# Spreading a row of reciprocal roots over the partitions: through DRAM instead of through TensorE

## The chip, the cores and the metric

The kernel runs on one core of one Trainium2 chip, as one launch. The metric is the device time of that core in microseconds, the median of several executions. One further execution is taken with the hardware profiler; its rows are what is read here. PE is TensorE (PEld its weight loads), DVE is VectorE, ACT is ScalarE, POOL is GpSimd, and SPq is the queue on which SyncE issues transfers.

## The reference, cut to what matters

Two layers of a transformer trunk, with 1024 tokens and a width of 1024, in float32. In each layer three groups of heads attend in their own ways, and each group's output is normalised by itself before the output projection:

```python
for l in range(DEPTH):
    h = rms_norm(x, g_attn[l]) * (1 + sc_a) + sh_a
    qa, ka, va, qb, kb, vb, qc, kc, vc = split_cols(h @ w_in[l], IN_SPLITS)
    ya = neighborhood_attention(...)       # 4 heads, two-dimensional window
    yb = sliding_window_attention(...)     # 6 heads, a band of 128 either way
    yc = axial_attention(...)              # 6 heads, dense
    ga, gb, gc = split_cols(g_group[l], GROUP_WIDTHS)      # widths 256, 384, 384
    y = jnp.concatenate([rms_norm(ya, ga), rms_norm(yb, gb), rms_norm(yc, gc)], axis=-1)
    x = x + gt_a * (y @ w_o[l])
    ...                                    # SwiGLU part, then the next layer

def rms_norm(x, g):
    y = x * lax.rsqrt(jnp.mean(x * x, axis=-1, keepdims=True) + EPS)
    return y * g
```

## The kernel before, in words

Features lie on the 128 partitions and tokens along the free dimension. The attention output is the tile `y`, eight chunks of 128 features by 1024 tokens: chunks 0 and 1 are the two-dimensional group, 2 to 4 the band group, 5 to 7 the dense group. A group's norm needs one factor per token, the same on all partitions.

The attention part is a list of 64 pairs (a head and two blocks of 128 queries): 24 dense ones, 16 of the two-dimensional group, 24 of the band group. A loop over the step `n` works on several pairs at once. For the last 40 pairs, which this text calls the attention band, step `n` computes the scores of pair `n`+4 (PE into `sA` or `sB`; DVE adds the bias from `zA` or `bz` and takes the extreme into `rs`), the exponentials of the pair scored a step earlier (ACT), the division of the one before that (`scale_rows` on `pr`, POOL), turns pair `n` by PE transposes into `T` (copied out as `pt` and `edge`), and multiplies pair `n`-2 with the values into `pv`. Two pairs share one `pv`; ACT copies half of it to `cmb` and DVE adds both into `y`, so DVE writes `y` once per two pairs.

A norm goes along beside that. As heads end, POOL squares and sums (`norm_sum`: `gsq` into `gss`). A list `later` holds callables by step. When a group's last head is done, at step `n` (24 for the dense group, 42 for the two-dimensional one), `stats` is put at `n`+5: PE sums `gss` over the partitions into `ps_st`, and DVE takes the reciprocal root by Newton steps (`isq`), which leaves `rstd`, 128 x 8: token 128j + p in column j of partition p. At `n`+8 `scale` calls `norm_scale`: for each half of 512 tokens `spread` transposes four columns of `rstd`, broadcast to 128 x 128, into one PSUM bank (`ps_r`), and ACT copies it to `rb`, 128 x 512, with the same row on each partition. The multiplies of `y` by `rb`, one per chunk and half, are put one per step from `n`+9, on POOL: six for the dense group, four for the two-dimensional one. The band group's norm comes after the loop and goes through the same `norm_scale`.

What orders the work: on PE, ACT and DVE the loop's own instructions are pinned, which means that they are held in written order; POOL is pinned throughout the loop; what `later` issues on PE, ACT and DVE is not pinned, and from step 6 SP isn't either. What is not pinned is placed by the framework's planner, which takes it up when it expects it to be ready. Each queue then executes in the order that was planned.

The transfers on SP in the band: the heads' `q` and `k` from `qkd` into `qk` tiles (two buffers). Group 0 of the band group is made in step 32 and group 1 in step 36, with five transfers of 512 KB each, when the `qk` tile of a head of the two-dimensional group comes free. The bias tiles `bz` come one per head, and the rows of `w_o` for the projection that follows (`wst`). Near the end of the band, `y_split` (ACT and DVE, into `yq`, a `qk` tile) makes two-part copies of scaled chunks, and parts of the projection (`ps_o`) are mixed in.

All instructions of the trace carry line 49, that of the helper that records them, so they are told apart by their tiles.

Of the kernel before, what the change touches and what calls it, by code (L numbers as in the profile page):

```python
# [10 lines left out]
F32 = mybir.dt.float32  # L11
# [3 lines left out]
ALU = mybir.AluOpType  # L15
# [4 lines left out]
P = 128  # L20
D = 1024
S = 1024
KC = D // P
H = 512
# [56 lines left out]
def bc(ap, shape):  # L81
    return ap.to_broadcast(shape)
# [3 lines left out]
def trunk(ctx: ExitStack, tc, A, C, out):  # L86
    nc = tc.nc
    pe, act, dve, pool, sp = (
        Engine(tc, e) for e in (nc.tensor, nc.scalar, nc.vector, nc.gpsimd, nc.sync)
    )  # L90
# [5 lines left out]
    def open_pool(name, bufs=1, side="left", space=None):  # L96
        kw = dict(name=name, bufs=bufs, side=side, reuse_waits="tile")
        if space is not None:
            kw["space"] = space
            if space == PSUM:  # L100
                kw.pop("side")
        cm = tc.tile_pool(**kw)
        p = cm.__enter__()
        return cm, p
# [10 lines left out]
    dp = ctx.enter_context(tc.tile_pool(name="dram", bufs=1, space=DRAM))  # L115
# [23 lines left out]
    skA = [dp.tile([4, P, 512], F32, name=f"skA{l}") for l in range(2)]  # L139
    vAd = dp.tile([S, 4 * P], F32, name="vAd")  # L140
    rowB = dp.tile([6, 512], F32, name="rowB")
    skB = dp.tile([6, P, 512], F32, name="skB")

    gpd = dp.tile([P, 7 * NB, H], F32, name="gpd")
# [177 lines left out]
    todo = [(0, g) for g in (2, 3, 4, 5)] + [(1, g) for g in range(6)]  # L322
# [114 lines left out]
    def spread(r, j0, psp, tag="mm"):  # L437

        ps = psp.tile([P, 512], F32, name="ps_r", tag=tag)
        for j in range(4):  # L440
            pe.transpose(
                ps[:, j * P : (j + 1) * P], bc(r[:, j0 + j : j0 + j + 1], [P, P]), ident
            )
        return ps
# [406 lines left out]
    rb = stp2.tile([P, H], F32, name="rb", tag="rb", bufs=2)  # L851
# [116 lines left out]
    rb = stp2.tile([P, H], F32, name="rb", tag="rb", bufs=2)  # L968
# [37 lines left out]
    for l in range(2):  # L1006
# [403 lines left out]
        for oc in range(NE, 8):  # L1410
            w = wab
            for half in range(2):
# [16 lines left out]
                i = 2 * (oc - NE) + half  # L1429
# [17 lines left out]
        y = yp.tile([P, 8, S], F32, name="y")  # L1447
        ap_cm, app = open_pool("apad", side="right")
        pad(app, 32)
        at_cm, atp = open_pool("att", side="right")  # L1450
        psT_cm, psT = open_pool("psT", bufs=PS_T, space=PSUM)
# [276 lines left out]
        class PairA(Band):  # L1728


            name, by_columns = "sA", True
# [11 lines left out]
        class PairB(Band):  # L1743
            name = "sB"
# [12 lines left out]
        def norm_sum(chunks, ss, last, half, late):  # L1757
# [14 lines left out]
            square(sq)  # L1772
            pool.tensor_tensor(out=ss[:, c], in0=ss[:, c], in1=sq, op=ALU.add)

        def norm_scale(chunks, r, psp, tag, engines):

            todo = []
            for half, eng in enumerate(engines):
                c = slice(half * H, (half + 1) * H)
                ps = spread(r, 4 * half, psp, tag=tag)  # L1780
                rb = atp.tile([P, H], F32, name="rb", tag="rb", bufs=2)
                act.copy(rb, ps)
                for n in chunks:
                    todo.append(
                        lambda eng=eng, n=n, c=c, rb=rb: eng.tensor_tensor(
                            out=y[:, n, c], in0=y[:, n, c], in1=rb, op=ALU.mult
                        )
                    )
            return todo

        korder = (5, 6, 7, 0, 1, 2, 3, 4)
# [59 lines left out]
        later = {}  # L1851
# [6 lines left out]
        for n in range(-AHEAD - 1, N + 3):  # L1858
# [84 lines left out]
            for end, (chunks, width) in norms.items():  # L1943
                if begins[end] <= m <= end and (m - begins[end]) % 8 == 7 and (n <= NC or m >= NC):
                    i = (m - begins[end]) // 8
                    if end not in gss:
                        gss[end] = gss_tile()
                    for half in range(2):
                        what = lambda a=(chunks, gss[end], i, half, m == N - 1): norm_sum(*a)
                        if m == N - 1:  # L1950
                            what()
                        else:
                            later.setdefault(n + 1 + half, []).append(what)
                    if m == end and end < N - 1:

                        def stats(end=end, width=width, n=n, chunks=chunks):
                            r = rstd_cols(
                                gss[end], width, 8, atp, psT, tag="T", newton=True, turned=False
                            )

                            def scale():
                                todo = norm_scale(chunks, r, psT, "T", (pool, pool))
                                for i, what in enumerate(todo):
                                    later.setdefault(n + 9 + i, []).append(what)

                            later.setdefault(n + 8, []).append(scale)

                        later.setdefault(n + 5, []).append(stats)
            pin((pe, act, dve), n < 0 or n >= NC - 1)
# [33 lines left out]
        for ki in range(5):  # L2003
# [8 lines left out]
            if ki == 2:  # L2012
                r = rstd_cols(gss[N - 1], norms[N - 1][1], 8, atp, psl, newton=True, turned=False)
# [316 lines left out]
        for q in range(NF):  # L2330
# [4 lines left out]
            if q < EARLY:  # L2335
                up = q % 2
                e = sg[q // 2][0][:, 0:H]
                if up:
                    (pool if q > 1 else dve).tensor_tensor(
                        out=e, in0=e, in1=quads[q]["11"], op=ALU.mult  # L2340
# [196 lines left out]
        for u in range(NU):  # L2537
            i, t = divmod(u, NB)
# [34 lines left out]
            if t < NB - 1:  # L2573
                continue
            m, half = {
                1: (0, 0), 2: (0, 0), 6: (0, 1), 7: (1, 1), 4: (1, 0), 5: (1, 1), 3: (0, 1),
            }[num]
# [29 lines left out]
        if last_layer:  # L2607
# [5 lines left out]
            r = ntp.tile([P, 8], F32, name="rstd", tag="rstd", bufs=2)  # L2613
# [122 lines left out]
```

## Time and profile before

| | us |
|---|---|
| median of 3 runs | 2355.33 (2355.26 to 2355.58) |
| profiled execution, time | 2355.82 |
| its span, first to last instruction | 2354.0 |
| granted TensorE clock, mean | 0.999 |
| `ps_r` transposes, `rstd` and identity, x72 | 0.273 each |
| copies `rb` from `ps_r` on ACT, x14 | 0.587 each |
| multiplies of `y` by `rb` on POOL, x26 | 1.290 each |

The span is what the rows add up to; the profiled execution took 1.8 us more than its span. Of the 72 transposes, 48 belong to the three group norms of two layers (eight each). A timeline row gives the start, the duration, the engine, the operation, the written and read tiles, the shapes and, in brackets, the idle time before it and what ended that. A row of a stretch gives the length, the busy time of PE, PEld, DVE, ACT and POOL with the number of instructions, the granted clock, the mean busy share of the 16 DMA engines, and the GB/s. A row of a transfer's tile view gives the minimum, median and maximum duration of its issue in ns, and the line under it the time from issue to landing. Layer 0's attention band lies at about 357 to 465 us of the span, layer 1's at about 1508 to 1616.

### The profile page before, as it was taken

To read this page: it belongs to the slowest core of one execution; us is meant where nothing else is said; L and a number is where in the kernel's file an instruction comes from. 1 tells how busy PE (TensorE), PEld (TensorE's weight loads), DVE (VectorE), ACT (ScalarE), POOL (GpSimd) and SP (SyncE) were. 2 spreads that over 40 slices of the span, in tenths; PEclk is the share of its full clock that TensorE was granted. 3 is DMA by queue.
4 is the path that set the end of the run, shared out by engine and by line. 5 is a ranking of instruction groups with operands and counts; after the bars stand their busy time and mean duration, and the time that the engine had idled before them with its cause. 6 is when DMAs were issued, how large, how long until landed. Compare 5 with 4: busy or idle time off the path is not lost. (4 is left out here: it accounts for less than half of the span.)

```text
span 2354.0 us, 33488 instructions
## 1 busy us (share of the span) xinstructions
PE 2320.3 (99%) x11825; PEld 1956.5 (83%) x11825; DVE 1737.0 (74%) x2720; ACT 1185.5 (50%) x2264; POOL 792.0 (34%) x758
## 2 busy tenths in 40 slices
PE   9999999999999999999999999999999999999998
PEld 7888898888788888888888889988878888888887
DVE  7866998869867777495777579897796664537865
ACT  5423888845543333344633168896454333334444
POOL 1530447610344444100145124574005443430021
PEclk9999999999999999999999999999999999999999
DMA  8676316163435444785434851332633443339633
GB/s 282 182 224 220 120 30 190 44 219 94 137 131 166 157 139 152 216 249 181 152 102 140 252 175 28 93 104 94 216 103 128 150 156 103 103 99 295 215 112 121
DMA packets 306168, 357.49 MB, mean 152 GB/s; under 512 B 51892, under 2 KB 223772, under 8 KB 306000
## 3 DMA queue, kind: packets, MB, share of 16 engines
q1 hardware_dynamic: 289504, 345.74, 46.5%
q10 hardware_dynamic: 16128, 9.44, 1.5%
q8 instruction: 93, 1.52, 0.3%
q14 instruction: 75, 0.61, 0.1%
q0 software_dynamic: 368, 0.17, 0.0%
HBM read 270.32 MB, written 88.63 MB: 152 GB/s over the span
## 5 line engine op out<-in xcount | busy, mean ns | idle before, releaser
L49 PE MATMUL ps_d<-wpt 128*128 128x512 f32 x1848 | 425.2, 390 | 0.8 <-ACT hh L49 0.2
L49 PEld LDWEIGHTS ps_d<-wpt 128*128 128x128 f32 x1848 | 345.4, 188 | 75.4 <-issue 1.9
L49 POOL TENSOR_SCALAR pr<-pr,rs 128x1024 f32<-128x1024 f32 (+2 forms) x248 | 190.8, 784 | 189.4 <-DVE rs L49 172.2
L49 POOL TENSOR_TENSOR sg<-sg,u 128x512 f32<-128x512 f32 x82 | 118.7, 1447 | 344.1 <-ACT sg L49 219.8
L49 PE MATMUL pv<-pt,vs 128*128 128x256 f32 x1088 | 174.0, 296 | 14.4 <-DVE y L49 13.1
L49 ACT COPY u<-ps_w 128x512 f32<-128x512 f32 x128 | 75.1, 587 | 213.5 <-PE ps_w L49 213.5
L49 DVE TENSOR_TENSOR pt<-T,pt 128x512 fp32r<-128x512 f32 x272 | 177.3, 679 | 7.0 <-ACT pt L49 5.8
L49 POOL TENSOR_TENSOR wpt<-ws,wpt 128x512 fp32r<-128x512 f32 x80 | 110.8, 1386 | 205.2 <-ACT wpt L49 152.0
L49 ACT CAST pt<-T 128x512 fp32r<-128x512 f32 x272 | 151.6, 586 | 42.3 <-PE T L49 40.9
L49 DVE TENSOR_TENSOR wpt<-w,wpt 128x512 fp32r<-128x512 f32 x154 | 110.3, 717 | 79.8 <-ACT wpt L49 79.6
L49 PEld LDWEIGHTS pv<-pt,vs 128*128 128x128 f32 x1088 | 141.0, 189 | 27.2 <-DVE y L49 25.2
L49 ACT CAST wpt<-w 128x512 fp32r<-128x512 f32 x154 | 95.6, 620 | 132.2 <-PE ps_d L49 124.7
L49 PE MATMUL T<-identr,pr 128*128 128x128 f32 x1176 | 159.9, 273 | 1.0 <-DVE pt L49 0.6
L49 PEld LDWEIGHTS T<-identr,pr 128*128 128x128 f32 x1176 | 137.8, 140 | 15.7 <-ACT edge L49 1.0
L49 DVE SCALAR_TENSOR_TENSOR acc<-wmt,condT,acc 128x512 f32<-128x512 f32 (+1 forms) x92 | 104.8, 1149 | 62.0 <-DMA wmt<-in_w_mod_dram 61.6
L49 ACT CAST wpt<-ws 128x512 fp32r<-128x512 f32 x176 | 107.2, 619 | 56.5 <-PE ps_w L49 26.7
L49 ACT CAST wpt<-graw 128x512 fp32r<-128x512 f32 x154 | 95.0, 617 | 72.5 <-DMA graw<-gpd 68.4
L49 DVE TENSOR_TENSOR wpt<-ws,wpt 128x512 fp32r<-128x512 f32 x96 | 83.1, 873 | 53.1 <-ACT wpt L49 52.8
L49 DVE TENSOR_TENSOR wpt<-graw,wpt 128x512 fp32r<-128x512 f32 x154 | 112.0, 727 | 11.7 <-ACT wpt L49 11.7
L49 DVE TENSOR_REDUCE rs<-sC 128x1 f32<-128x1024 f32 x88 | 107.4, 1220 | 12.7 <-PE sC L49 11.5
L49 DVE TENSOR_TENSOR ws<-wr 128x512 f32<-128x512 f32 x88 | 81.8, 930 | 41.3 <-POOL wpt L49 38.0
L49 DVE TENSOR_TENSOR wlo<-wst,whi 128x1024 fp32r<-128x1024 f32 (+1 forms) x71 | 92.6, 1308 | 25.1 <-ACT whi L49 21.7
(314 smaller groups left out, 5943.1 us busy)
## 6 DMA issues: line engine op xcount, KB each, us to landing
wr<-in_w_gu_dram SPq DMA_DIRECT2D x92, 512.0 KB, 4.1
gpd<-sg SPq DMA_DIRECT2D x154, 256.0 KB, 4.4
graw<-gpd SPq DMA_DIRECT2D x76, 512.0 KB, 3.5
w<-in_w_down_dram SPq DMA_DIRECT2D x110, 256.0 KB, 4.7
wmt<-in_w_mod_dram SPq DMA_DIRECT2D x48, 512.0 KB, 5.2
qk<-qkd SPq DMA_DIRECT2D x44, 512.0 KB, 7.2
wst<-in_w_o_dram SPq DMA_DIRECT2D x32, 512.0 KB, 4.2
wmt<-in_w_mod_dram SPq DMA_DIRECT2D x64, 256.0 KB, 3.9
```

What stands on the lines that cost most here:

```text
L49: ins = op(*args, **kwargs)
```

## The change

For the dense and the two-dimensional group, `rstd` no longer goes through PE, PSUM and ACT. At `n`+8 SP stores it to a DRAM row of 1024 elements (`rowN`), at `n`+9 SP loads each half of that row to all 128 partitions of an `rb` tile, and the multiplies, still on POOL, are put from `n`+12. The band group's norm keeps `norm_scale`.

```diff
     rowB = dp.tile([6, 512], F32, name="rowB")
+    rowN = dp.tile([S], F32, name="rowN")
...
+        def scaled(chunks, half, rb, eng):
+
+            c = slice(half * H, (half + 1) * H)
+            return [
+                lambda n=n: eng.tensor_tensor(
+                    out=y[:, n, c], in0=y[:, n, c], in1=rb, op=ALU.mult
+                )
+                for n in chunks
+            ]
+
+        def rb_tile():
+            return atp.tile([P, H], F32, name="rb", tag="rb", bufs=2)
+
         def norm_scale(chunks, r, psp, tag, engines):
 
             todo = []
             for half, eng in enumerate(engines):
-                c = slice(half * H, (half + 1) * H)
                 ps = spread(r, 4 * half, psp, tag=tag)
-                rb = atp.tile([P, H], F32, name="rb", tag="rb", bufs=2)
+                rb = rb_tile()
                 act.copy(rb, ps)
...
+                todo += scaled(chunks, half, rb, eng)
+            return todo
+
+        def rows_store(r):
+            sp.dma_start(rowN.rearrange("(j p) -> p j", p=P), r)
+
+        def rows_load(chunks):
+            todo = []
+            for half in range(2):
+                rb = rb_tile()
+                row = rowN[half * H : (half + 1) * H]
+                sp.dma_start(rb, bc(row[None, :], [P, H]))
+                todo += scaled(chunks, half, rb, pool)
             return todo
...
                             def scale():
-                                todo = norm_scale(chunks, r, psT, "T", (pool, pool))
-                                for i, what in enumerate(todo):
-                                    later.setdefault(n + 9 + i, []).append(what)
-
-                            later.setdefault(n + 8, []).append(scale)
+                                for i, what in enumerate(rows_load(chunks)):
+                                    later.setdefault(n + 12 + i, []).append(what)
+
+                            later.setdefault(n + 8, []).append(lambda: rows_store(r))
+                            later.setdefault(n + 9, []).append(scale)
```

More of the change, by code (lines that the diff above doesn't have):

```diff
@@ L1778, in norm_scale @@
             for half, eng in enumerate(engines):
-                c = slice(half * H, (half + 1) * H)
                 ps = spread(r, 4 * half, psp, tag=tag)
-                rb = atp.tile([P, H], F32, name="rb", tag="rb", bufs=2)
+                rb = rb_tile()
                 act.copy(rb, ps)
[L1783 to L1788, printed above, removed]
+                todo += scaled(chunks, half, rb, eng)
[9 more added lines that the diff above has]
+                todo += scaled(chunks, half, rb, pool)
             return todo
```

## The prediction

> **What bounds the kernel now.** I read the page first (engines, chain, DMA queues), then the busy time by stretch around the places that change, then the order of events there.
>
> ```profile
> span 2354.0 us, 33488 instructions
> ...
> PE 2320.3 (99%) x11825; PEld 1956.5 (83%) x11825; DVE 1737.0 (74%) x2720; ACT 1185.5 (50%) x2264; POOL 792.0 (34%) x758
> ...
> q1 hardware_dynamic: 289504, 345.74, 46.5%
> q10 hardware_dynamic: 16128, 9.44, 1.5%
> ```
>
> TensorE is busy for 99% of the span, so over the whole program it is the bound, and any TensorE work that goes away can shorten it. The span average hides the attention band, though, where the edit lies:
>
> ```profile
> core 0: us, PE busy (x) PEld busy (x) DVE busy (x) ACT busy (x) POOL busy (x), PEclk, DMA share, GB/s
> 381.00:390.50 9.50, 9.11 (x72) 8.44 (x71) 8.11 (x29) 8.95 (x25) 6.82 (x10) 1.00 0.94 275
> 391.50:400.60 9.10, 8.64 (x67) 8.05 (x66) 8.15 (x26) 8.77 (x26) 9.10 (x15) 1.00 0.97 283
> 425.00:437.00 12.00, 9.34 (x75) 8.70 (x73) 11.76 (x32) 11.77 (x32) 9.55 (x13) 1.00 0.07 19
> ```
>
> At the first norm (chunks 5 to 7) PE and ACT are nearly full, and ten microseconds later POOL is full without a gap. The DMA engines are also full through both stretches. At the second norm (chunks 0 and 1) DVE and ACT are full, PE isn't, and DMA is idle. So the four places (two norms in two layers) have two different prices.
>
> **What is removed.** Per changed norm, two halves of four transposes and one copy:
>
> ```profile
> L49 PE MATMUL ps_r<-identr,rstd x8: 271/273/273, 384.0 to 384.8; 128*128 128x128 f32 x8
> L49 ACT COPY rb<-ps_r x2: 575/584/592, 384.7 to 385.2; 128x512 f32<-128x512 f32 x2
> ...
> 384.02 1.04 PE L49 MATMUL ps_r<-identr,rstd 128*128 128x128 f32 x8
> 428.57 1.04 PE L49 MATMUL ps_r<-identr,rstd 128*128 128x128 f32 x8
> 1535.54 1.04 PE L49 MATMUL ps_r<-identr,rstd 128*128 128x128 f32 x8
> ```
>
> That is 1.04 us of PE for eight pipelined transposes (with their eight weight loads beneath) and about 1.06 us of ACT, four times in all. What a place is worth can be read from the beat of the loop. DVE writes one `y` per two pairs:
>
> ```profile
> 381.89 0.69 DVE L49 TENSOR_TENSOR y<-pv,cmb 64x512 f32<-64x512 f32 x1
> 387.46 0.69 DVE L49 TENSOR_TENSOR y<-pv,cmb 64x512 f32<-64x512 f32 x1 [0.20 <-ACT cmb L49]
> 391.99 0.68 DVE L49 TENSOR_TENSOR y<-pv,cmb 64x512 f32<-64x512 f32 x1
> 396.68 0.68 DVE L49 TENSOR_TENSOR y<-pv,cmb 64x512 f32<-64x512 f32 x1 [0.19 <-ACT cmb L49]
> ```
>
> The beats are 5.57, 4.53 and 4.69 us; the first contains the transposes. Against the mean of the other two (4.61) it is 0.96 us long, so nearly all of the 1.04 us is on the path: gain 0.95 at the first norm. One pair (one step `n`) is thus 2.3 us. At the second norm DVE is busy 11.76 of 12.00 us, so taking work from PE and ACT can give no more than DVE's free 0.24 us as long as DVE's own work stays; the other end would be the full 1.04. I take 0.2, since DVE is the nearer limit. Over two layers: 2 x 0.95 + 2 x 0.2 = 2.3 us gained if nothing new is waited for.
>
> **What is added.** Four stores (1024 elements of 4 bytes each, strided) and eight loads (128 partitions x 2 KB, all from one row) on SP, 12 issues. A store waits for `rstd`; both loads wait for the store to land, and whatever SP holds behind them waits too. The multiplies by `rb` stay on POOL, same count and size, but three steps later (`n`+12 for `n`+9). POOL's order is fixed, so a late `rb` also holds the divisions of `pr` that stand behind it, and PE's transposes of `pr` wait for those. What is just then on the DMA queue is the heart of it:
>
> ```profile
> 383.73 0.16 DVE L49 SCALAR_TENSOR_TENSOR rstd<-isq,rstd 128x8 f32<-128x8 f32 x1
> ...
> L49 SPq DMA_DIRECT2D qk<-qkd x5: 430/580/598, 379.8 to 382.1; - x5
> DMA to landing us min/median/max: 4.8/9.1/9.8
> ...
> L49 SPq DMA_DIRECT2D qk<-qkd x5: 430/580/607, 389.8 to 392.2; - x5
> DMA to landing us min/median/max: 5.1/7.4/8.1
> ...
> L49 SPq DMA_DIRECT2D qk<-qkd x5: 430/580/609, 1531.3 to 1533.7; - x5
> DMA to landing us min/median/max: 5.0/7.0/8.6
> ...
> L49 SPq DMA_DIRECT2D qk<-qkd x5: 430/579/614, 1541.3 to 1543.7; - x5
> DMA to landing us min/median/max: 6.2/8.8/9.6
> ...
> bz<-skB SPq DMA_DIRECT2D x12, 192.0 KB, 2.3
> skB<-rowB SPq DMA_DIRECT2D x6, 256.0 KB, 10.3
> ```
>
> `rstd` is ready at 383.9. The five 512 KB loads of group 0 were issued from 379.8 to 382.1 and land one after another, the last 9.8 us after 382.1, at 391.9: the later the issue, the longer the landing, which is a queue served in order. I take it that the store, issued at 384 on the same queue, lands behind them. Its own transfer isn't in the trace. Queue q1's packets took 46.5% of 16 x 2354 us for 289504, or 60.5 ns each (mean 1.2 KB), q10's 1.5%, or 35 ns each (585 B). With 1024 packets over 16 engines that is 64 x 60.5 = 3.9 us at the upper end and next to nothing at the lower; nearest are q10's small packets, 2.2 us, and since 4 B is far less than 585 B I take half, 1.1. So the store lands at 393.0. Then a load: the quiet 192 KB `bz` took 2.3 us, and 256 KB at that rate of growth some 2.6 (upper end: the broadcast `skB` loads, six in a row, 10.3). So `rb` is there at L = 395.6.
>
> The Trainium skill (DMA: Bandwidth & Descriptors, Rules for kernel authors) says that a strided last dimension becomes one descriptor per element, and its Measured table gives about 10.5 ns a packet: 64 x 10.5 = 0.67 us, an estimate, which would put the sum below 0.4 us lower in each layer. No run here shows such a store.
>
> **When POOL needs it.**
>
> ```profile
> 385.38 1.29 POOL L49 TENSOR_TENSOR y<-y,rb 128x512 f32<-128x512 f32 x1 [0.20 <-ACT rb L49]
> 390.58 0.18 POOL L49 COPY pr<-sinkc 128x2 f32<-128x2 f32 x1
> 391.98 1.03 POOL L49 TENSOR_TENSOR gss<-y 128x512 f32<-128x512 f32 x1
> 400.05 1.28 POOL L49 TENSOR_TENSOR y<-y,rb 128x512 f32<-128x512 f32 x1
> 401.32 1.15 POOL L49 TENSOR_SCALAR pr<-pr,rs 128x384 f32<-128x384 f32 x2
> ...
> 390.97 0.83 PE L49 MATMUL sB<-qk 128*128 128x256 f32 x4
> 403.79 0.81 PE L49 MATMUL T<-identr,pr 128*128 128x128 f32 x6
> 410.20 0.71 PE L49 MATMUL T<-identr,pr 128*128 128x128 f32 x5
> ```
>
> A step costs POOL 1.1 (division) + 0.18 (sink) + 1.29 (multiply) = 2.6 us against a beat of 2.3, so POOL falls behind while the multiplies last; a division is used two steps later. Now the sixth multiply's next division ends at 401.32 + 1.15 = 402.5 for a transpose of pair 41 at 403.79: 1.3 us to spare, no more. After the change the train of six multiplies starts three steps later. From its first start at L, POOL does 6 multiplies, one `gss` and 6 divisions with 5 sinks before the last division it delays: 7.7 + 1.0 + 6.6 + 0.9 = 16.2 us. That one belongs to pair 44, transposed at 410.20, or 409.2 with 0.95 taken off. So L may be 393.0. (The first sB at 390.97 is pair 40, scored at step 36; counting on gives the pairs.) At 395.6 PE stalls 2.6 us. In layer 1 everything stands 1151.5 later (1535.54 against 384.02), but group 0's last load lands at 1533.7 + 8.6 = 1542.3 instead of 1543.4, 1.1 earlier: stall 1.5.
>
> At the second norm DMA is at a share of 0.07: store from 428.6, 2.6 + 2.6 us plus issues, `rb` near 435. Its multiplies start at step 54, four steps after the store's step, some 9 us: hidden. The `bz` load queued beside it has ten steps before its own use. Group 1's loads behind the first norm's wait are used from step 48, and are late without harm. Were these covers gone, it would cost the same microsecond for microsecond.
>
> **Sum.** -2.3 + 2.6 + 1.5 = +1.8 us. The profiled execution took 2355.82 around a span of 2354.0, 0.5 above the median of 2355.33 (2355.26 to 2355.58); on the median it gives 2357.1. About 0.2% (4.7 us) is what a measurement here can tell from no change, so this is no change.
>
> **Rivals.**
>
> *The loads stand behind group 1 on SP (slower).* SP's order is set ahead by a planner. Group 1 is free to go at 389.8, before the store has landed (393.0); if the planner sees that, its five loads go first. For it: ready first. Against it: the `rb` loads come three steps earlier in the program. Then L is group 1's last landing, 392.2 + 8.1 = 400.3, less 0.95, plus about 1 for the load itself: 400.4, a stall of 7.4; in layer 1, 1553.3 + 0.05 against 1544.5: 8.9. Sum 16.3 - 2.3 = +14.0, 2369.3. It decides from the point where group 1's first issue precedes the `rb` loads.
>
> *The small writes are slow (slower).* At 60.5 ns a packet the store takes 3.9 instead of 1.1, L grows by 2.8 in both layers, +1.8 + 5.6 = +7.4: 2362.7. For it: nothing in this trace writes 4-byte pieces. Against it: smaller packets are cheaper in the two queue rows. The Trainium skill (DMA: Bandwidth & Descriptors, Specifications) speaks for this one: below 512 B it says the engine reads, modifies and writes. No run here shows it.
>
> *The transfers are hidden (no change).* If the store is not held by group 0, it lands about 387 and `rb` about 390, before 393.0: -2.3, 2353.0; with the whole 1.04 at the second norms too, -4.0, 2351.3. Against it: the rising landing times.
>
> *More than the removed work comes back (faster).* If both the PE and the ACT microsecond lie on the path at all four places, because the planner lays out the unpinned splits around 425 anew, 4 x 2.1 = 8.4: 2346.9. Against it: DVE at 11.76 of 12.00.
>
> **How the numbers follow.** My forecast 0.32, hidden 0.20, behind group 1 0.24, slow writes 0.12, more comes back 0.12. The likeliest gives 2357.1, its own range 2354 to 2360. Faster by over 0.2% is only the last: 0.12. Slower is the two slow ones plus a little of my own range's upper part: 0.38. The rest, 0.50, is within. The range for 8 in 10 leaves out the faster case and the far end of the slow one: 2350.5 to 2371.
>
> **What would show it.** Right: the transposes and copies of `rstd` are gone at four places of six; the beat at 381.9 falls to 4.6; the store lands 8 to 9 us after its issue in the first norms and 2 to 4 in the second; POOL waits for DMA `rb` about 4 us once per layer, and PE's T waits for POOL `pr`, 2.6 and 1.5 us. Wrong: no wait of POOL for `rb` (hidden), one of some 9 us with group 1 issued ahead (behind group 1), or a store that lands long after group 0 (slow writes). Gains elsewhere would mean a new layout by the planner, which I can't read from this trace.

## The result, and the profile after

The changed kernel takes 2390.72 us, the median of 4 runs (2386.55 to 2393.56), where the kernel before, timed beside it on the same chip, takes 2355.30 (2355.07 to 2355.58). The ratio is 1.0147, with a 95% interval of 1.0135 to 1.0158: 35 us slower. I had forecast 2357.1, no change, in a range that ended at 2371.0. The profiled execution took 2388.63 around a span of 2386.4, 32.4 more than the span before; the accounts below are made on the spans.

The page after, its span and its engines:

```profile
span 2386.4 us, 33424 instructions
...
PE 2326.6 (97%) x11793; PEld 1962.3 (82%) x11793; DVE 1734.2 (73%) x2720; ACT 1182.6 (50%) x2256; POOL 793.0 (33%) x758
```

PE has 32 instructions fewer and is busy a little longer (2326.6 us, 2320.3 before); it stands idle for 60 us of the span instead of 34. So 26 of the 32.4 us are waiting. What SyncE's queue issued in layer 0, around the two changed norms (start, duration, queue):

```profile
384.29 0.37 SPq L49 DMA_DIRECT2D rowN<-rstd  x1
389.30 0.58 SPq L49 DMA_DIRECT2D qk<-qkd  x1
398.56 2.45 SPq L49 DMA_DIRECT2D rb<-rowN  x2
...
438.00 0.37 SPq L49 DMA_DIRECT2D rowN<-rstd  x1
447.08 0.32 SPq L49 DMA_DIRECT2D rb<-rowN  x1
```

The store of the dense norm's factors was issued at 384.29, where I had put it. The two loads of `rb` could only be issued once it had landed, and that was at 398.56, not at 393.0. One of group 1's `qk` loads went between; the other four went behind. At the second norm the same store takes from 438.00 to 447.08, 9.1 us, for 4 KB (in layer 1 from 1605.99 to 1616.63, 10.6 us). Busy time by stretch after (columns as in the prediction):

```profile
402.00:406.00 4.00, 0.24 (x1) 0.24 (x2) 0.00 (x0) 0.00 (x0) 3.12 (x4) 0.50 0.94 185
438.00:440.00 2.00, 2.00 (x19) 2.00 (x18) 2.00 (x7) 2.00 (x6) 1.31 (x4) 1.00 0.23 2
440.00:441.00 1.00, 1.00 (x11) 0.97 (x9) 0.91 (x5) 0.97 (x4) 1.00 (x2) 1.00 0.00 0
...
452.00:456.00 4.00, 0.33 (x1) 0.18 (x1) 0.98 (x3) 2.91 (x8) 4.00 (x6) 0.92 0.04 14
```

The second row is the second store at work: 0.23 of 2 us on 16 engines is 1024 packets of 4 bytes at 7 ns each, and the trace has all of them between 438.91 and 439.59. From 440 to 441 the DMA share is 0.00, and yet the store lands only at 447.0. So its packets take 0.7 us, and the 7.4 us behind the last of them, which show as no DMA work, are what the loads wait for. Other transfers are slow beside it: two packets of 8 KB on another queue that start in that time (441.4 and 442.5) take 3.06 us each, where two such packets took 0.31 and 0.49 us in the kernel before (433.1 and 433.8). The first and the last row show what the late stores cost: from 402 to 406 and from 452 to 456, PE did 0.24 and 0.33 us of work in 4 us. The order of events there, at the first norm:

```profile
402.88 1.26 POOL L49 TENSOR_TENSOR y<-y,rb 128x512 f32<-128x512 f32 x1 [10.37 <-DMA rb<-rowN]
...
405.76 1.36 PE L49 MATMUL T<-identr,pr 128*128 128x128 f32 x5 [7.29 <-POOL pr L49]
...
418.58 0.84 PE L49 MATMUL sB<-qk 128*128 128x256 f32 x4
```

POOL waited 10.37 us for `rb`, and PE behind it 7.29 us for the division `pr` that stands behind the multiply in POOL's order. The row `sB` at 418.58 is pair 48. Before, the same pair, pair 52 and the first product of the output projection that reads `y` stood here:

```profile
409.53 0.83 PE L49 MATMUL sB<-qk 128*128 128x256 f32 x4
...
420.53 0.84 PE L49 MATMUL sB<-qk 128*128 128x256 f32 x4
...
507.19 0.39 PE L49 MATMUL ps_o<-y,whi 128*128 128x512 f32 x1
```

So layer 0's first norm costs 418.58 - 409.53 = 9.05 us. And the second norm after, with the same product:

```profile
451.77 1.26 POOL L49 TENSOR_TENSOR y<-y,rb 128x512 f32<-128x512 f32 x1 [5.04 <-DMA rb<-rowN]
...
453.07 0.72 ACT L49 ACTIVATE qk<-y,vecs 128x512 fp32r<-128x512 f32 x1 [5.34 <-POOL y L49]
...
455.67 0.47 PE L49 MATMUL T<-identr,pr 128*128 128x128 f32 x1 [4.92 <-ACT edge L49]
...
522.56 0.39 PE L49 MATMUL ps_o<-y,whi 128*128 128x512 f32 x1
```

POOL waits 5.04 us for `rb`; ACT waits 5.34 us for POOL's product `y`, because the split of that chunk (`qk<-y,vecs`) stands in ACT's order ahead of work that the loop needs; PE waits 4.92 us for ACT's `edge`. By that product layer 0 has lost 522.56 - 507.19 = 15.37 us, so the second norm's share is 6.3. Layer 1 repeats it, first before, then after:

```profile
1561.04 0.84 PE L49 MATMUL sB<-qk 128*128 128x256 f32 x4
```

```profile
1570.85 1.26 POOL L49 TENSOR_TENSOR y<-y,rb 128x512 f32<-128x512 f32 x1 [11.01 <-DMA rb<-rowN]
...
1573.72 1.36 PE L49 MATMUL T<-identr,pr 128*128 128x128 f32 x5 [7.93 <-POOL pr L49]
...
1586.52 0.83 PE L49 MATMUL sB<-qk 128*128 128x256 f32 x4
```

Pair 48 of layer 1 is 25.48 us late, 10.1 more than layer 0 had lost; the last product of the projection that reads `y` in layer 1 is 31.4 late (1703.17 before, 1734.57 after). That accounts for 9.05 + 6.3 + 10.1 + 5.9 = 31.4 of the 32.4 us.

### The profile page after: what moved, and what is told of

The parts are those of the page before. It is cut to its first block, busy times and chain, and to the rows that moved or that the text cites. A ratio compares the mean times of both kernels' runs of the same rounds, so it can differ in the third digit from the quotient of the medians.

```text
span 2386.4 us, 33424 instructions
## 1 busy us (share of the span) xinstructions
PE 2326.6 (97%) x11793; PEld 1962.3 (82%) x11793; DVE 1734.2 (73%) x2720; ACT 1182.6 (50%) x2256; POOL 793.0 (33%) x758
## 4 chain that ended last, share of the span: by engine, by line
PE 66%; DVE 6%; DMA 2%; issue 2%; POOL 1%; ACT 1%; SPq 1%; ACTq 0%; DVEq 0%; POOLq 0%
PE ps_w L49 33%; PE ps_d L49 12%; PE ps_o L49 7%; PE ps_ab L49 3%; PE pv L49 3%; PE T L49 2%; PE ps_v L49 2%; PE sC L49 2%; DMA w<-in_w_down_dram 1%; DVE wpt L49 1%; SPq L49 1%; DVE w L49 1%; DVE xb L49 1%; POOL pr L49 1%; PE ps_c L49 1%
## 5 line engine op out<-in xcount | busy, mean ns | idle before, releaser
L49 DVE TENSOR_TENSOR wpt<-graw,wpt 128x512 fp32r<-128x512 f32 x154 | 112.0, 727 | 12.2 <-ACT wpt L49 12.1
L49 PE MATMUL ps_w<-ht4h,wpt 128*128 128x512 f32 x352 | 108.6, 390 | 1.6 <-ACT u L49 1.6
L49 PE MATMUL ps_w<-h22h,wpt 128*128 128x512 f32 x352 | 108.8, 390 | 1.0 <-ACT sg L49 1.0
```

Of the source, the lines that this page charges most:

```text
L49: ins = op(*args, **kwargs)
```

## The experiments

Each diff is against the changed kernel unless the text says otherwise, and each ratio is to the kernel before on the same chip. "Until its load" means from the issue of the store to the issue of the first load of `rb`, which waits for it.

**The work removed, alone.** The kernel before, without transposes and copies; the multiplies use a column of ones, so the factors are left out. No store, no loads, no later multiplies.

```diff
-                                todo = norm_scale(chunks, r, psT, "T", (pool, pool))
+                                todo = [... pool.tensor_tensor(out=y[:, n, c], in0=y[:, n, c],
+                                            in1=bc(ones, [P, H]), op=ALU.mult) ...]
```

> The kernel before without the transposes and copies of the two norms: y is multiplied by a column of ones spread by its access pattern, at the same steps on POOL; so the norm factors of the dense and the two-dimensional group are left out. It shows what the removed work is worth if nothing is waited for. Prediction's step: 0.95 us at each first norm and 0.2 at each second, 2353.0. Rival (PE and ACT time both on the path at all four places): 2347. Rival (all hidden): 2355.3.

2354.35 us, 0.9989 (0.9979 to 0.9998): 2.6 us, with an interval of 0.5 to 4.9, against 2.3 in the prediction. With the multiplies where they are, this bounds what any way of spreading the factors can win. The rows divide the gain otherwise than I had. Pair 57, just behind the second norm, before and then here:

```profile
434.90 0.94 PE L49 MATMUL sB<-qk 128*128 128x384 f32 x4
```

```profile
433.17 0.95 PE L49 MATMUL sB<-qk 128*128 128x384 f32 x4
```

It comes 1.73 us earlier, while pair 52, just ahead of that norm, stands level (420.53 before, 420.57 here). At the last pair of the band some 1.2 us of it are left (449.21 and 448.06), and in layer 1 about as much. The first norm of layer 0 gives 0.9 us by pair 40.

**Each norm alone.** The spread through DRAM for one group, `norm_scale` at `n`+9 for the other.

```diff
+                            if end == 23:        # the other run: 39
                                 later.setdefault(n + 8, []).append(lambda: rows_store(r))
                                 later.setdefault(n + 9, []).append(scale)
+                            else:
+                                later.setdefault(n + 8, []).append(scale_old)
```

> Store and loads for the dense group's norm alone, the two-dimensional group as before. From the changed kernel's rows the first norms cost 7.3 and 7.9 us of TensorE stall and about 2.6 us each of work at half clock behind it, less 0.95 each: +18.5, ratio 1.0078. If the second norms are the larger part, below 1.006.

> Store and loads for the two-dimensional group's norm alone. The rows show 4.9 and 5.2 us of stall behind ACT's y_split, 1.3 and 1.7 behind y, some 2.5 each at half clock: +13 to +14, ratio 1.0057. My prediction's step (hidden cover at the second norms): 1.000.

The dense norm alone: 2378.18 us, 1.0088 (1.0072 to 1.0103). The two-dimensional norm alone: 2369.15, 1.0048 (1.0033 to 1.0063). They add up to 1.0136, against 1.0147 for both. The part that I had called hidden costs a third of the loss. Its rows:

```profile
443.95 1.26 POOL L49 TENSOR_TENSOR y<-y,rb 128x512 f32<-128x512 f32 x1 [5.88 <-DMA rb<-rowN]
...
445.25 0.72 ACT L49 ACTIVATE qk<-y,vecs 128x512 fp32r<-128x512 f32 x1 [4.66 <-POOL y L49]
...
447.85 0.48 PE L49 MATMUL T<-identr,pr 128*128 128x128 f32 x1 [4.93 <-ACT edge L49]
```

The three waits of the second norm are there without the first norm's change, so they are its own.

**Another queue for the store.**

```diff
-            sp.dma_start(rowN.rearrange("(j p) -> p j", p=P), r)
+            act.dma_start(rowN.rearrange("(j p) -> p j", p=P), r)
```

> The changed kernel with the store issued from ACT's queue, the loads still from SP. Theory A (the store is slow by itself, as the second norms show where nothing else moves: 9.1 us from issue to the load's issue): the first norms' store takes about 9 instead of 14.3 us, POOL waits about 5 instead of 10.4, TensorE still stalls 2 to 3 us there, the second norms don't change: 2372 to 2380. Theory B (it waits behind group 0 on SP's queue): the store lands 2 to 3 us after its issue, no wait at the first norms, 2370 or less from them alone. If ACT's queue shares the lines fully with SP's: no change, 2389.

2388.31 us, 1.0134 (1.0119 to 1.0149). The second norm's store went from ScalarE's queue at 437.54 and its load at 446.82: 9.3 us, on another queue. There it isn't what SyncE holds in front. At the first norm the store took 12.8 us (384.03 to 396.81), not the 9 that theory A expected: its packets start 4.5 us after its issue there and 0.9 us after it at the second norm. So group 0's loads hold it on ScalarE's queue too, and standing behind them in SyncE's order isn't the whole of that delay.

**Pieces of 32 bytes.** The same 4 KB, written as 128 pieces, one for each partition; the factors then belong to other tokens than those they multiply.

```diff
-            sp.dma_start(rowN.rearrange("(j p) -> p j", p=P), r)
+            sp.dma_start(rowN.rearrange("(p j) -> p j", j=8), r)
```

> The changed kernel with the store's row in the order of partitions, 128 pieces of 32 bytes instead of 1024 of 4; the factors then go to the wrong tokens. Theory A (4-byte pieces make the store slow): from issue to landing about 2.5 us in the second norms instead of 9, no POOL wait and no clock fall there; in the first norms it lands with the end of group 0, some 9 us after its issue instead of 14, and TensorE stalls about 2 to 3 us: 2357 to 2362. Theory B (order of the queue, not the pieces): 2385 to 2393 as before.

2363.94 us, 1.0031 (1.0020 to 1.0043): most of the loss is gone.

```profile
383.95 0.32 SPq L49 DMA_DIRECT2D rowN<-rstd  x1
...
393.50 0.80 SPq L49 DMA_DIRECT2D rb<-rowN  x2
...
397.27 1.29 POOL L49 TENSOR_TENSOR y<-y,rb 128x512 f32<-128x512 f32 x1 [5.09 <-DMA rb<-rowN]
...
412.98 0.84 PE L49 MATMUL sB<-qk 128*128 128x256 f32 x4
...
432.45 0.32 SPq L49 DMA_DIRECT2D rowN<-rstd  x1
433.88 0.32 SPq L49 DMA_DIRECT2D rb<-rowN  x1
```

At the second norm the store now takes 1.4 us until its load, and POOL waits for nothing there. At the first norm the load still goes only at 393.50, 9.6 us after the store: group 0's `qk` loads are in front, and that delay is the one that I had predicted (393.0).

**Half the pieces.** Only the first half is stored, 512 pieces of 4 bytes; both loads read it, so the second half of the tokens gets the first half's factors.

```diff
+            sp.dma_start(rowN[0:H].rearrange("(j p) -> p j", p=P), r[:, 0:4])
...
+                row = rowN[0:H]
```

> The changed kernel with half the store: four columns of rstd, 512 pieces of 4 bytes, and both halves of tokens multiplied with the first half's factors. If the store's time goes with its pieces (9.1 us for 1024 in the quiet second norms, 1.4 for 128 pieces of 32 bytes): about 5 us there, POOL's wait at the second norms about 1 us instead of 5, and at the first norms about 6 instead of 10.4; ratio about 1.007. If it is a fixed cost of 4-byte writes: 9 us and 1.0147.

2387.43 us, 1.0131 (1.0117 to 1.0145).

```profile
437.87 0.37 SPq L49 DMA_DIRECT2D rowN<-rstd  x1
446.17 0.32 SPq L49 DMA_DIRECT2D rb<-rowN  x1
```

8.3 us until its load instead of 9.1. Half the pieces save a tenth of the time, so no price per piece explains the store. The other theory, a fixed cost of 4-byte writes, came near (9 us and 1.0147 expected); the next two runs test it.

**The same pieces, apart.** 1024 pieces of 4 bytes again, but 64 bytes apart, or 512 bytes. The loads read the first 4 KB of the longer buffer, which hold other numbers than the factors; one more store, near 13 us of the span, fills them.

```diff
-            sp.dma_start(rowN.rearrange("(j p) -> p j", p=P), r)
+            wide = rowN.rearrange("(j p s) -> p j s", p=P, s=16)     # the other run: s=128
+            sp.dma_start(wide[:, :, 0], r)
```

> The same 1024 pieces of 4 bytes, each at a place of its own 64 bytes apart in a DRAM buffer 16 times as long; the loads read its first 4 KB (other factors than they should be). Theory A, that neighbouring 4-byte pieces that share a stretch of DRAM wait for each other: the second norm's store takes 1.5 to 3 us until its load is issued (437.9 to 441 at most) instead of 9.1, POOL doesn't wait for rb there, and the time is near that of the 32-byte pieces, some 2364 to 2368. Theory B, that it is the count or the size of the pieces: still 8 to 9 us, and 2388 to 2391.

> As the run with 64 bytes, but the 4-byte pieces are 512 bytes apart in a buffer 128 times as long. Theory A with a stretch of up to 512 bytes: 1.5 to 3 us and some 2364 to 2368, whatever the run with 64 bytes gives. Theory B: 8 to 9 us, and 2388 to 2391.

64 bytes apart: 2362.47 us, 1.0028 (1.0018 to 1.0038). 512 bytes apart: 2361.63, 1.0021 (1.0012 to 1.0031). With 64 bytes (the last row is busy time by stretch):

```profile
398.70 1.26 POOL L49 TENSOR_TENSOR y<-y,rb 128x512 f32<-128x512 f32 x1 [5.95 <-PE sB L49]
...
414.40 0.84 PE L49 MATMUL sB<-qk 128*128 128x256 f32 x4
...
433.84 0.37 SPq L49 DMA_DIRECT2D rowN<-rstd  x1
436.50 0.32 SPq L49 DMA_DIRECT2D rb<-rowN  x1
...
434.00:436.00 2.00, 2.00 (x19) 2.00 (x18) 2.00 (x9) 2.00 (x7) 1.48 (x4) 1.00 0.23 2
```

(The first row's bracket names `sB`, but the first load of `rb`, issued at 394.37, landed 4.3 us later, which is when POOL starts.) At the second norm it is 2.7 us until the load with 64 bytes, and 2.4 with 512 (433.40 to 435.82), with the same number of pieces of the same size. The packets run as in the changed kernel: the share is again 0.23, and the trace has all 1024 between 434.74 and 435.42. The difference lies behind the last packet: the store lands 1.0 us after it, at 436.45, where the changed kernel's needs 7.4. So neither the count nor the size made the store slow: 4-byte neighbours did. In the changed kernel, neighbouring addresses belong to neighbouring partitions, and pieces that share a stretch of up to 64 bytes seem to be written one after another; the number that share a stretch is the same for 512 pieces as for 1024, which fits the 8.3. How long a stretch is (over 4 and up to 64 bytes), and what passes between two neighbours, these runs don't show.

**Later multiplies.** The dense and the two-dimensional norm's multiplies from `n`+15.

```diff
-                                    later.setdefault(n + 12 + i, []).append(what)
+                                    later.setdefault(n + 15 + i, []).append(what)
```

> The changed kernel with the multiplies put at n+15 instead of n+12. Theory: all of the loss is lateness of rb (there at 402.9 us in the first norm of layer 0 and 451.8 in the second, against a first multiply wanted at about 392.5 and 446.7), and the fall of the granted clock to 0.5 is a consequence of the idle TensorE. Three steps are about 7 us: the first norms keep a wait of POOL of 3 to 4.5 us and a TensorE stall of 3 to 4.5, the second norms none; the clock stays at 1.00 throughout. Time 2355.3 - 2.3 + about 7 = 2360. Rival (the loss is the transfers themselves, by contention or by holding SP): as the changed kernel, 2385 to 2393.

2380.01 us, 1.0100 (1.0085 to 1.0115), a miss: I had thought that three steps would cover the store. POOL still waits 5.5 us for `rb` at the first norm. At the second POOL no longer waits for a transfer, but ACT's split now waits 2.3 us for the later product instead; moving the multiplies moves the wait. In layer 0 TensorE loses 3.7 us by pair 48, 2.8 more by pair 52 and 5.4 more between pair 56 and the first product that reads `y`, so most of the loss here is not the wait for `rb`.

**An order of tokens that makes the 32-byte pieces right.** The sums over features are taken for every eighth token, so that a partition holds eight neighbours, with multiplies from `n`+15.

```diff
+                src = ssq.rearrange("p (t j) -> p j t", j=8)[:, j, :] if step else ...
+                pe.matmul(ps[:, j : j + 1], src, ones, start=True, stop=True)
...
+            sp.dma_start(rowN.rearrange("(p j) -> p j", j=8), r)
```

> The changed kernel with three edits that keep the result: the sums over partitions take every eighth token (ps_st column j of partition p is token 8p + j), so the store is 128 contiguous pieces of 32 bytes in token order; and the multiplies at n+15. Theory (pieces make the store slow, lateness makes the loss, the planner's hoisted y_split and the clock follow from it): store 1.4 us at the second norms, about 9.5 at the first, rb there by about 398, wanted at about 399; no wait of POOL for rb above 1 us, clock 1.00 throughout, time that of the kernel before less the 2.5 us that leaving the transposes out gave: ratio 0.999. Rival (transfers on SP cost something of their own): ratio 1.000 to 1.002.

2382.08 us, 1.0107 (1.0092 to 1.0122), a miss: slower than the 32-byte pieces with multiplies from `n`+12. POOL no longer waits for `rb`; part of the loss is the reading of weights with a step of 8, and the later multiplies of both norms are in it too. The rows of layer 0 separate them in part. The first norm's 16 sums take 3.86 us (1.84 in the changed kernel), and pair 40, ahead of any multiply, is 3.33 us late where the changed kernel had it 0.48 early. Between pair 56 and the first product that reads `y` 4.4 us more are lost; there the run above lost 5.4 with plain weights, and 32-byte pieces with the two-dimensional multiplies at `n`+12 (further down) 0.3, so this goes with the later two-dimensional multiplies. The weight loads of the sums here, then in the changed kernel:

```profile
L49 PEld LDWEIGHTS ps_st<-onesr,gss x96: 188/334/336, 375.6 to 1653.9; 128*128 128x128 f32 x96
```

```profile
L49 PEld LDWEIGHTS ps_st<-onesr,gss x96: 186/192/192, 375.4 to 1660.0; 128*128 128x128 f32 x96
```

334 ns instead of 192, and a second price behind it, in this kernel's busy time by stretch:

```profile
380.00:384.00 4.00, 4.00 (x22) 3.97 (x21) 2.70 (x12) 2.06 (x6) 1.15 (x2) 0.58 0.01 5
```

PE counts as busy for all of the 4 us, yet its granted clock, right behind the sums, is 0.58.

**A turned store, later.** One transpose of the 128x8 factors and a small ACT copy, then a store of 8 rows of 512 bytes; dense multiplies from `n`+15, two-dimensional ones from `n`+12.

```diff
+            T = t_tile()
+            pe.transpose(T[:8, 0, :], r, ident)
+            rT = atp.tile([8, P], F32, name="rT", tag="rT", bufs=1)
+            act.copy(rT, T[:8, 0, :])
+            sp.dma_start(rowN.rearrange("(j p) -> j p", p=P), rT)
```

> A version with the same result that should lose nothing: rstd (128 x 8) is turned by one TensorE transpose and one small ACT copy to 8 x 128, stored as 8 contiguous rows of 512 bytes, loaded as in the changed kernel; multiplies at n+15 for the dense group, n+12 for the two-dimensional one. Theory: store to load issue 1.5 to 2.5 us at the second norms, some 9 at the first, no POOL wait for rb above 1 us, clock 1.00: ratio 0.999 to 1.000 (the 2.5 us of the transposes and copies won, less about 0.4 us at each of four places for the turn). Rival (any dependence of POOL and of the hoisted splits on two transfers in a row costs, as in the stepped version): 1.003 or more.

2359.93 us, 1.0016 (1.0007 to 1.0025).

```profile
385.61 0.29 SPq L49 DMA_DIRECT2D rowN<-rT  x1
...
391.27 0.80 SPq L49 DMA_DIRECT2D rb<-rowN  x2
...
399.69 1.29 POOL L49 TENSOR_TENSOR y<-y,rb 128x512 f32<-128x512 f32 x1
```

The store lands 5.7 us after its issue with group 0 still in front, and POOL multiplies without a wait. Nearly all of the loss is gone, and yet nothing is won: the time is still above that of the kernel before, clear of noise, and neither theory had it. Three more runs ask where the gain of 2.6 us stays.

> The store is made of 128 pieces of 32 bytes (the factors come to other tokens than they belong to), and the dense norm's multiplies start at n+15. Theory A, that a store and two loads that are in time cost nothing: no wait of POOL for rb in any of the four places, and the 2.3 to 2.6 us of the removed work are gained, 2352.5 to 2353.5, 0.999. Theory B, that the later multiplies cost by themselves what the removed work gave, as in the run with the turned store (1.0016): 2356 to 2359.

(32-byte pieces, no turn, the same places for the multiplies.) 2357.55 us, 1.0005 (0.9996 to 1.0015).

```profile
398.85 1.30 POOL L49 TENSOR_TENSOR y<-y,rb 128x512 f32<-128x512 f32 x1
...
408.44 0.84 PE L49 MATMUL sB<-qk 128*128 128x256 f32 x4
...
417.83 1.00 PE L49 MATMUL T<-identr,pr 128*128 128x128 f32 x5 [0.72 <-POOL pr L49]
...
421.55 0.83 PE L49 MATMUL sB<-qk 128*128 128x256 f32 x4
```

No wait for `rb`; pair 48 stands at 408.44, 1.09 us earlier than before, so the first norm's gain is there. But pair 52 stands at 421.55, 1.02 later than before: 2.1 us went again in between. The last multiply, three steps later than before, now stands on POOL beside the squares of the next group, and PE waits for POOL's `pr` (0.72 us at 417.83) and, a step earlier, for DVE's `y` (0.76 us at 415.57).

> As the run with the store turned to 8 rows of 512 bytes, with the dense norm's multiplies from n+14 instead of n+15. With 32-byte pieces and n+15 the first norm gained 1.1 us (pair 48 at 408.44 against 409.53) and lost 2.1 right behind, where the last multiply stands on POOL beside the second norm's squares (TensorE waited 0.7 us for pr at 417.83, pair 53 at 421.55 against 420.53). Theory A, that this collision is what n+15 costs: one step earlier it goes, some 2 us per layer come back less the 1 us by which rb may now be late, 2355 to 2358, 0.9995 to 1.0005. Theory B, that rb lands at about 397.5 and n+14 is too early: POOL waits 1 to 2 us for it in each first norm, and the time stays at 2360, 1.0016.

> The same, for the dense norm alone; the two-dimensional norm is as before. Theory A: the second norms' part is near nothing either way (0.4 us gained by the removed work, as predicted), so the time is that of the run with both within 1 us. Theory B, that the turned store costs at the second norm, where DVE has no slack: faster than the run with both by 1 to 3 us.

(The turned store with the multiplies from `n`+14; the second for the dense norm alone. The pair that the expectation calls 53 is pair 52, counted from 40.) 2358.37 us, 1.0008 (0.9999 to 1.0017), and 2356.75, 1.0002 (0.9993 to 1.0011).

```profile
409.11 0.83 PE L49 MATMUL sB<-qk 128*128 128x256 f32 x4
...
420.93 0.83 PE L49 MATMUL sB<-qk 128*128 128x256 f32 x4
```

Here pair 48 gains 0.42 and pair 52 loses 0.40: part of the collision is gone, part of the gain too. The first time is between the two theories; the second is 1.6 us below it, as theory B of that run has it, but within the intervals. Both intervals overlap with those of `n`+15; which lead is best isn't settled. No version that spreads the factors through DRAM was faster than the kernel before.

**Was the fall of the clock a cost?** In the changed kernel PE's clock stands at 0.50 behind the idle time (the first row by stretch above). Idle products were put in step 39 to keep PE at work, 28 and then 38.

```diff
+                if n == 39:
+                    fill = t_tile()
+                    for _ in range(28):          # the other run: 38
+                        pe.matmul(fill, identr, bc(identr[:, None, :], [P, 4, P]), ...)
```

> The changed kernel with 28 idle matrix products (identity, 128x512, result unused) on TensorE in step 39, ahead of the transposes that wait in the first norms; they take about 6.4 us of the 7.3 and 7.9 us there. Theory (the clock falls because TensorE idles, and the fall costs about 2.6 us a time): clock 1.00 behind the first norms' stall, 5 us faster than the changed kernel, ratio to the kernel before 1.0125. Rival (the clock falls for another reason, or its fall is hidden since others are late anyway): as the changed kernel, 1.0147, or slower by the products.

> The changed kernel with 38 instead of 28 idle products in step 39, some 8.9 us, so that TensorE hardly idles before the division arrives (28 left 2.2 us idle and the clock still fell). Theory (idle TensorE lowers the clock, and the lower clock costs): clock 1.00 behind the first norms, 4 to 5 us faster than the changed kernel, ratio 1.012 to 1.013. Rival (the clock doesn't matter there): 1.0147 or more.

With 28: 2388.73 us, 1.0138 (1.0121 to 1.0155); they left 2.16 us idle, the clock fell to 0.52, and nothing follows. With 38: 2390.19, 1.0145 (1.0131 to 1.0158).

```profile
402.00:406.00 4.00, 4.00 (x19) 3.29 (x19) 0.00 (x0) 0.00 (x0) 0.00 (x0) 1.00 0.85 154
```

The clock now holds at 1.00. Then the first multiply and pair 48:

```profile
406.40 1.30 POOL L49 TENSOR_TENSOR y<-y,rb 128x512 f32<-128x512 f32 x1 [11.76 <-DMA rb<-rowN]
...
422.14 0.83 PE L49 MATMUL sB<-qk 128*128 128x256 f32 x4
```

From the first multiply to pair 48 it takes 15.74 us, with the full clock; in the changed kernel 418.58 - 402.88 = 15.70, with 0.50 of it until 410 and 0.88 from 410 to 414. POOL sets the pace there, busy without a gap, and the slower clock is hidden. For the first norms my theory that the clock was part of the loss fell; at the second norms it wasn't tested.

**Was it the split on ACT or POOL's lateness, at the second norm?** The two-dimensional norm alone, with the splits of chunks 7, 0 and 1 held behind the loop; and the kernel before with the same hold, as its partner.

```diff
+                pin((act, dve), True)
                 for i in range(2, 5):
                     y_split(korder[i], 0, yq[:, i, 0:H], yq[:, i, H:S])
+                pin((act, dve), False)
```

> Store and loads for the two-dimensional group alone (ratio 1.0048 before), and the two-part copies of chunks 7, 0 and 1 held on ACT and DVE behind the loop's last instruction, where the program writes them, so that the planner can't put them among the band's work. Theory (ACT waits in one of these copies for POOL's late y, and with it the edge copies that TensorE needs): no wait of ACT for y and none of TensorE's T for the edge copy of 4.9 us in the band; a POOL wait of about 5 us for rb stays, of which TensorE sees 0 to 2. The copies come later, so the projection after the loop may wait a few us for them; ratio 1.001 to 1.004. Rival (POOL's late division alone stalls TensorE): the stall stays at 4 to 5 us, 1.005 or more.

> This is the kernel before with the splits of chunks 7, 0 and 1 held behind the loop, the partner of the run that changed the two-dimensional norm alone with the same splits held (1.0071 of before). Theory A, that the late multiplies on POOL and not the hoisted split carry the second norm's loss: holding the splits costs the kernel before some 0.1 to 0.2% (1.001 to 1.002), so that 0.5% remains for the store and loads, as much as without holding (1.0048). Theory B, that the hoisted split carries it: holding costs the kernel before some 0.6% (1.006 or more), and what remains for the store and loads is 0.1% or less.

2373.30 us, 1.0071 (1.0057 to 1.0085), and 2366.52, 1.0045 (1.0028 to 1.0062). The wait for `rb` in the first of the two, from 440 to 460 us (who waits for whom, us in total, times, longest):

```profile
POOL y L49 <- DMA rb<-rowN: 6.5, 1, 6.5
```

The wait of ACT for `y` is gone, POOL's 6.5 us for `rb` is not. Against its partner the norm now costs 1.0071 / 1.0045 = 1.0026, with an interval of about 0.0022 either way (the two widths added as squares), where it cost 1.0048; the two differ by less than their intervals can tell. Neither theory came out clean: some of the loss remains without the hoisted split, and how it divides is not settled.

## Why the prediction was wrong, point by point

*The gain* (2.3): the sum agrees with the 2.6 measured (0.5 to 4.9), in part by luck. The first norm was right: 0.9 in layer 0 with the work removed alone, where I had said 0.95, and pair 48 came 1.09 earlier in a run without waits. The second norm was not: I had taken 0.2, because DVE had 0.24 us free, and some 1.2 are left there at the end of the band. DVE's busy share was no bound on what TensorE could gain.

*The queue in front of the store*: the delay was right where the store itself is quick. With 32-byte pieces the load could go at 393.50; I had 393.0. With the turned store it could go at 391.27, and the last load of group 0 was to land at 391.9. The reason that I gave, one queue served in order, is not the whole: on ScalarE's queue the store still took 3.5 us longer at the first norm than at the second (12.8 and 9.3). Nor do the two times add up as in my sum: 7.9 us behind group 0 and 9.1 for the store would be 17.0, and the changed kernel took 14.3.

*The store's own transfer* (1.1, at most 3.9): this is the first step that failed. It is 9.1 us at the second norm, with nothing in front. I had priced it by the time a packet takes in two queue rows. The packets were not what was slow: all 1024 took 0.7 us. What I had put at nothing, without a reason, is the time from the last packet to the landing, and that is 7.4 us when the 4-byte pieces are neighbours and 1.0 us when they lie 64 bytes apart. No packet price could have shown it. The estimate that I drew from the Trainium skill (DMA: Bandwidth & Descriptors, Measured table), 0.67 us, agrees with the 0.7 us of the packets and leaves out the landing as well. The rival that I called slow writes came nearest, but it priced packets too, and small writes as such are not slow here. The Trainium skill (DMA: Bandwidth & Descriptors, Specifications) says that below 512 B the engine reads, modifies and writes; pieces of 4 bytes 64 bytes apart fall under that too and took 2.7 us, so the rule alone doesn't give 9.1.

*The load* (2.6): 402.88 - 398.56 = 4.3 us to the first multiply, beside group 1, and 451.77 - 447.08 = 4.7 at the second norm. That is the smaller miss. `rb` came at 402.88 where I had 395.6, of which 5.6 us is the store and 1.7 the load.

*How POOL passes lateness on* (PE stalls by L - 393.0, less 0.95): right, at three values of L. 402.88 gives 8.9 (measured 9.05), 397.27 gives 3.3 (412.98 - 409.53 = 3.45), 398.70 gives 4.75 (414.40 - 409.53 = 4.87). Put in with the right L, the step would have said +9 for layer 0 instead of +1.6.

*The second norms* (hidden, -0.2 each): the second step that failed. I had written that without the cover it would cost the same microsecond for microsecond; the cover was nine microseconds, the transfers took 451.77 - 438.00 = 13.8 from the store's issue, and POOL waited 5.04. PE lost 6.3. I had looked at who waits for POOL's multiplies in the loop and not at the split on ACT, which the planner had put ahead of the loop's own work.

*SP's order*: the rival with all of group 1 ahead of the loads did not come; one of its five went ahead. The rival that the transfers are hidden was the opposite of what happened.

Term by term, in us over both layers, with the gain inside each term: first norms +4.1 - 1.9 = +2.2 (measured 9.05 + 10.1 = +19.2); second norms -0.4 (measured 6.3 + 5.9 = +12.2). The sum was +1.8, and the spans differ by 32.4.

## What to carry to other kernels

A store that scatters single 4-byte values to neighbouring addresses is a latency of some 9 us here (9.1 for 4 KB, 8.3 for 2 KB), nearly all of it after its packets have run, so that an idle DMA row doesn't show it: before it takes the place of a few transposes, give each partition a contiguous run, or turn the tile first, and ask what is ahead of it on the queue. When an operation of the change isn't in the trace at all, rows of other transfers don't bound it, a packet's time is not a landing, and the range should reach to where the wait would hurt. An in-order engine passes a late operand to everything behind it, so look on every engine for what stands behind the operation that may be late, the scheduler's hoisted work included.

## What the runs showed of the hardware that I had not expected

- The store of 4 KB from 128 partitions, until its load: 9.1 us as 1024 neighbouring pieces of 4 bytes, 8.3 as 512 (2 KB), 2.7 and 2.4 as 1024 pieces 64 and 512 bytes apart, 1.4 as 128 pieces of 32 bytes. With neighbours and 64 bytes apart alike, 1024 packets ran in 0.7 us; the landing came 7.4 us after the last packet with neighbours, 1.0 us when they lay 64 bytes apart.
- While the store of neighbours was landing, two 8 KB packets of another queue took 3.06 us each instead of 0.31 and 0.49.
- Weight loads whose columns lie eight elements apart took 334 ns instead of 192, and TensorE's granted clock fell to 0.58 behind sixteen of them, as behind idle time, though the engine counted as busy.
- A granted clock of 0.50 from 402 to 410 us cost nothing measurable where POOL set the pace: 15.70 us against 15.74 with the full clock.
